# Delta stage of a fused two-block transformer: eight scalings and eight products from VectorE to GpSimd, four key-head projections and two transposes into other PSUM banks

## Chip, cores and metric

The kernel runs on one core of one Trainium2 chip. The metric is the device time of one execution in microseconds (us). Each core has engines that run their own instruction lists in order: TensorE (PE: matmuls and transposes through the PE, with its weight loads as PEld), VectorE (DVE), ScalarE (ACT), GpSimd (POOL) and SyncE (SP), which here issues nearly all DMAs. A matmul writes to one of eight PSUM banks, and VectorE or ScalarE must read a bank out before it is written again.

## The reference

The kernel computes two transformer blocks on 256 tokens of width 1024. The change touches only the last layer, a gated DeltaNet mixer, on 272 positions (16 meta positions ahead of the 256):

```python
def deltanet_mixer(h, norm_w, w_in, conv_w, a_log, dt_bias, o_norm_w, w_out):
    u = rms_norm(h, norm_w) @ w_in
    qkv, z, b, a = jnp.split(u, ...)
    qkv = jax.nn.silu(causal_depthwise_conv(qkv, conv_w))
    ...
    q = jnp.repeat(l2_norm(q...), rep, axis=2)
    k = jnp.repeat(l2_norm(k...), rep, axis=2)
    q = q * (DN_HEAD_DIM_K ** -0.5)
    beta = jax.nn.sigmoid(b)
    g = -jnp.exp(a_log) * jax.nn.softplus(a + dt_bias)
    o = chunked_gated_delta_rule(q, k, v, beta, g)
    o = rms_norm(o, o_norm_w) * jax.nn.silu(z)
    return o @ w_out
```

There are 8 key heads, 8 query heads and 16 value heads of 128. The recurrence runs in chunks: the 16 meta positions, then two chunks of 128 tokens. Each chunk needs, for each value head, the inverse of a unit triangular matrix of 128x128 made of the key products and the decays.

## The kernel before

All of this happens in `delta()`, the last stage, from about 1160 us to the end of the span. Layouts are transposed: features on the 128 partitions, positions along the free axis.

**Projections.** The input projection is cut into 49 weight blocks, here called units. Unit 0 gives the rates b and a, units 1 to 8 the key heads, 9 to 16 the query heads, 17 to 32 the value heads, 33 to 48 the gates z. For each unit `unit()` loads a 128x1024 block (`raw`, a ring of four), splits it into a rounded half `hi` on ScalarE (L269) and a rest `lo` on VectorE (L270; rings of three, so that the halves of unit k+3 wait until TensorE is done with unit k), and `proj_t` runs 24 matmuls (lines L280, L281, L282 in turn) into one bank, `pj_ps`. Units 1 to 8 multiply the unnormalised halves `hh`, `hl`, and their result is scaled afterwards by the row R of reciprocal norms when it is read out (`cpad`, L1310, VectorE). For the others `normalise(k)` makes normalised halves `nh`, `nl` meanwhile: `nt` = h times R (L1253, VectorE), then `split_scaled` (L325 on ScalarE, L326 on VectorE).

**Heads.** `conv_head` reads a unit out, applies a causal convolution of four taps (for key heads one tap goes through ScalarE and a GpSimd addition, L1323; the others are VectorE operations, L1325), and `silu` follows on ScalarE (L1330). `gates` evicts the units 33 to 48 with a silu straight from the bank (`z`, also L1330). The tiles of the raw value heads (`craw`) are two buffers, and the gate tiles `z` reuse them: the gates of units 37 to 40 go where the raw value heads 12 to 15 were.

**Chunks.** `decay`, `between` and `products` make the decays and key products; `attend(c, h0)` multiplies the decays by the queries (L1480) and the key-query products. `values()` also transposes, for four value heads at a time, the raw heads (`tp`, L1571), their meta positions (`tp`, L1577, read out as `va`, L1579) and the meta keys (`tp`, L1582, read out as `ka`), and makes the state S after the meta chunk (`mv`, `vsA`, `mS`).

**Inverse.** `inverse()` is a generator whose steps are put between those of `values()`. It gathers the 32x32 diagonal blocks by way of DRAM (`ab`, L1491), inverts them by 31 steps of substitution on VectorE (`sb_t`, L1222, and `ub`, L1224), sends the result back through DRAM (`e<-ub`, L1496, and eight `U<-e`, L1499), and then, for each of eight groups of four heads, puts the blocks together on TensorE: transposes on VectorE (L1513), products `r` (L1519), `zt` and `z` (L1527, L1531), `r` (L1539), `z` (L1545), with evictions on ScalarE (`pr`, L1522 and L1533; `rn`, L1542) and copies on VectorE between them. `step` and `finish` then run the chunks and the output projection.

**PSUM.** Four pools of two banks each: `pj` (tag "pj") for the projections, `pa`, `pb` and `pk` (tag "b") for all else. Before the change both sorts of meta transposes take banks of `pb`, which also holds `kq`, `mv`, `mS`; `pk` holds `zt` and `z` of L1545, and some of the decays; `pa` holds the key products, `r`, and `z` of L1531.

**Order.** A scheduler orders each engine's list from the program and its own estimates; so an edit in one place can reorder many instructions elsewhere. Waits are then put in where an operation needs another engine's result or a free buffer.

Of the kernel before, what the change touches and what calls it, by code (L numbers as in the profile page):

```python
# [6 lines left out]
F32 = mybir.dt.float32  # L7
# [5 lines left out]
ALU = mybir.AluOpType  # L13
# [177 lines left out]
class Net:  # L191
# [1035 lines left out]
    def delta(self, NZ=2, AH=4, KN=8, SS=1, SR=3, SW=3):  # L1227
        nc, ap = self.nc, self.ap
        ident, tri = self.c("ident"), self.c("tri")
        conv = self.d("conv").rearrange("p (b i) -> p b i", i=4)  # L1230
        h4 = self.h3
        A = self.pool("deA", side="right")
        dr = self.pool("deD", space=bass.MemoryType.DRAM)
        pa = self.pool("pa3", bufs=2, space=PSUM, side="left")
        pb = self.pool("pb3", bufs=2, space=PSUM, side="left")
        pj = self.pool("pj3", bufs=2, space=PSUM, side="right")
        pk = self.pool("pk3", bufs=2, space=PSUM, side="right")
        bank = lambda p, n: p.tile([128, 4, 128], F32, name=n, tag="b")
# [11 lines left out]

        def normalise(k):
            t = W.tile([128, L], F32, name="nt", bufs=2)
            nc.vector.tensor_mul(t, h4[:, k], R)  # L1253
            self.split_scaled(nh[:, k], nl[:, k], t, gd[:, k:k + 1])

        def proj(ts=slice(0, L)):
            ps = pj.tile([128, 512], F32, name="pj_ps", tag="pj")
            n = ts.stop - ts.start
            u = next(units)
            a = (hh, hl) if u <= KN else (nh, nl)  # L1260
            self.proj_t(ps[:, :n], self.unit(ap["w_t3"][u]), (a[0][:, :, ts], a[1][:, :, ts]))
            return ps[:, :n]


        X = Slices(V.tile([128, 2048], F32, name="early", tag="8"))
        bt = X.tile([128, L], F32, name="bat")
        nc.vector.tensor_mul(bt, proj(), R)
        tp = bank(pb, "tp")
        for c in (1, 2, 0):
# [31 lines left out]
        def conv_head(dst, b, t0=0):  # L1301

            n = L - t0
            t = max(t0 - 4, 0)
            w = [conv[:, b, i:i + 1] for i in range(4)]
            ps = proj(slice(t, L))
            src = W.tile([128, L], F32, name="cpad", bufs=2)[:, :L - t]
            early = 8 <= b < 8 + KN
            if early:
                nc.vector.tensor_mul(src, ps, R)  # L1310
                ps = src
            else:
                nc.scalar.activation(src, ps, AF.Copy)
            nc.scalar.activation(dst, ps[:, t0 - t:t0 - t + n], AF.Copy, scale=w[3])  # L1314
            for i in (2, 1, 0):

                o = max(3 - i - t0, 0)
                at = t0 - t - 3 + i + o
                x, y = src[:, at:at + n - o], dst[:, o:]
                if early and i == 2:  # L1320
                    x2 = W.tile([128, L], F32, name="ctap", bufs=2)[:, :n - o]
                    nc.scalar.activation(x2, x, AF.Copy, scale=w[i])
                    nc.gpsimd.tensor_add(y, y, x2)  # L1323
                else:
                    nc.vector.scalar_tensor_tensor(y, x, w[i], y, op0=ALU.mult, op1=ALU.add)  # L1325

        def silu(raw, after=None, src=None):

            with self.tc.issue_after(self.last), self.tc.issue_after(after or self.last):
                return nc.scalar.activation(raw, raw if src is None else src, AF.Silu).ins  # L1330
# [21 lines left out]
        qT = A.tile([128, 8, T], F32, name="qT", tag="q8")  # L1352
# [56 lines left out]
        for j in range(8):  # L1409
            conv_head(kT[:, j], 8 + j)  # L1410
            normalise(j)
            if j == 2:
                cumulate()
            if j in (3, 5, 7):
                silu(kT[:, (0 if j == 3 else j - 1):j + 1])
# [9 lines left out]
        ps = pb.tile([128, 8, M], F32, name="mkk", tag="b")  # L1425
# [31 lines left out]
        for c in range(2):  # L1457
# [6 lines left out]
            for h0 in range(0, 16, 4):  # L1464
# [5 lines left out]
                                        op=ALU.mult)  # L1470
# [3 lines left out]
        def attend(c, h0):  # L1474
            ts = CH[c + 1]
            tq = slice(ts.start - M, ts.stop - M)
            hs = slice(h0, h0 + 4)
            j0 = h0 // 2
            q4 = qg[c][:, hs].rearrange("p (j r) c -> p j r c", r=2)
            nc.vector.tensor_tensor(q4, q4, qT[:, j0:j0 + 2, None, tq].to_broadcast([128, 2, 2, 128]), op=ALU.mult)  # L1480
            ps = bank(pb, "kq")
            for j in range(2):
                nc.tensor.matmul(ps[:, j], kT[:, j0 + j, ts], qT[:, j0 + j, tq], start=j == 0, stop=True,
                                 skip_group_check=True)
            a4 = at[c][:, hs].rearrange("p (j r) c -> p j r c", r=2)
            nc.vector.tensor_tensor(a4, a4, ps[:, 0:2, None, :].to_broadcast([128, 2, 2, 128]), op=ALU.mult)
# [68 lines left out]
        def values():  # L1555
            for j in range(8):
                conv_head(qT[:, j], j, M)
            v.extend(half("v", c) for c in range(2))
            for h0 in range(0, 16, 4):
                hs = slice(h0, h0 + 4)  # L1560
                raw = A.tile([128, 4, L], F32, name="craw", bufs=2)
                for j in range(4):
                    conv_head(raw[:, j], 16 + h0 + j)
                    if h0 and j % 2:
                        attend(j // 2, h0 - 4)
                    yield
                silu(qT[:, h0 // 2:h0 // 2 + 2], silu(raw))
                for c in range(2):
                    tp = bank(pb, "tp")
                    for j in range(4):  # L1570
                        nc.tensor.transpose(tp[:, j], raw[:, j, CH[c + 1]], ident)  # L1571
                    for j in range(0, 4, 2):
                        nc.scalar.activation(v[c][:, h0 + j:h0 + j + 2], tp[:, j:j + 2], AF.Copy,
                                             scale=ri[:, c + 1, (h0 + j) // 2:(h0 + j) // 2 + 1])
                tp = bank(pb, "tp")
                for j in range(4):
                    nc.tensor.transpose(tp[:M, j], raw[:, j, CH[0]], ident)  # L1577
                va = W.tile([M, 4, 128], F32, name="va")
                nc.scalar.activation(va, tp[:M], AF.Copy)  # L1579
                tp = bank(pb, "tp")  # L1580
                for j in range(2):
                    nc.tensor.transpose(tp[:M, j], kT[:, h0 // 2 + j, CH[0]], ident)  # L1582
                ka = W.tile([M, 2, 128], F32, name="ka")
                nc.scalar.activation(ka, tp[:M, 0:2], AF.Copy)
                ps = bank(pb, "mv")
                for j in range(4):
                    nc.tensor.matmul(ps[:M, j], um[:, h0 + j], va[:, j], start=True, stop=True,
                                     skip_group_check=True)
                vs = W.tile([M, 4, 128], F32, name="vsA")
                nc.vector.tensor_tensor(vs, ps[:M], bw[:M, 0, hs, None].to_broadcast([M, 4, 128]), op=ALU.mult)  # L1590
                ps = bank(pb, "mS")
                for j in range(2):
                    nc.tensor.matmul(flat(ps[:, 2 * j:2 * j + 2]), ka[:, j],
                                     flat(vs[:, 2 * j:2 * j + 2]), start=True, stop=True, skip_group_check=True)
                nc.scalar.activation(S[:, hs], ps, AF.Copy)
            for c in range(2):
                attend(c, 12)
                yield
            for h0 in range(0, 4 * NZ, 4):
                z = A.tile([128, 4, T], F32, name="z", tag="craw", bufs=2)  # L1600
                yield from gates(z)
                sz.append(z)
            self.logexp()

        def gates(z):
            for j in range(4):
                silu(z[:, j], src=proj(slice(M, L)))
                yield
# [4 lines left out]
        for _ in values():  # L1613
            next(side, None)
# [113 lines left out]
        op = [o0, o1]  # L1728
# [46 lines left out]
```

## Time and profile before

| | us |
|---|---|
| median of 3 runs | 1471.88 (1471.32 to 1475.75) |
| the profiled execution, its own time | 1471.34 |
| its span in the trace | 1468.7 |
| TensorE busy in the span | 1442.7 (98%) |
| VectorE busy | 1058.8 (72%) |
| ScalarE busy | 793.4 (54%) |
| GpSimd busy | 73.2 (5%) |

The time of the profiled execution is 2.64 us more than its span. Busy shares are over the whole span; the delta stage is the last fifth of it. Line numbers in the trace are those of the kernel; behind the change they are two higher from L1255 on (L1330 becomes L1332, L1513 becomes L1515).

### The profile page before, as it was taken

What the parts mean: (1) busy time and instruction counts of PE and PEld (TensorE: products, weight loads), DVE (VectorE), ACT (ScalarE), POOL (GpSimd) and SP (SyncE); (2) the same over time, 40 slices, a digit from 0 to 9 for tenths busy, and PEclk for the clock granted to TensorE, in tenths of its full rate; (3) what the DMA queues carried; (4) which work ended last, traced back from release to release, by engine and by line L of the source; (5) the groups of instructions that cost most, each with busy time, mean ns of one, the idle gap of its engine ahead of it and who ended that gap; (6) DMA issues with size and microseconds to landing.
All of it is one profiled execution on the core that took longest, in us unless ns stands there. A gap on an engine that the chain in (4) does not pass through costs nothing.

```text
span 1468.7 us, 27090 instructions
## 1 busy us (share of the span) xinstructions
PE 1442.7 (98%) x10635; PEld 1320.6 (90%) x10635; DVE 1058.8 (72%) x2114; ACT 793.4 (54%) x1364; POOL 73.2 (5%) x106
## 2 busy tenths in 40 slices
PE   9999999999999999999999999999999989999998
PEld 8788999999999999999888888888898989899786
DVE  7667577789948888998555555555777688885564
ACT  5566545545544444444444445445686667764464
POOL 0000000000000000000000000000113024000020
PEclk9999999999999999999999999999999999999999
DMA  7452464555665545555666656666442434545113
GB/s 241 131 158 73 146 193 150 171 164 170 198 177 159 161 154 172 157 150 172 191 195 193 194 190 204 190 195 190 154 119 87 144 115 140 164 128 158 33 57 102
DMA packets 72079, 229.19 MB, mean 156 GB/s; under 512 B 16032, under 2 KB 16192, under 8 KB 71952
## 3 DMA queue, kind: packets, MB, share of 16 engines
q1 hardware_dynamic: 71408, 225.82, 50.3%
q8 instruction: 83, 1.36, 0.4%
q0 software_dynamic: 400, 1.46, 0.3%
q14 instruction: 44, 0.36, 0.1%
q10 hardware_dynamic: 144, 0.20, 0.1%
HBM read 225.31 MB, written 2.13 MB: 155 GB/s over the span
## 4 chain that ended last, share of the span: by engine, by line
PE 93%; ACT 2%; DVE 2%; issue 1%; DMA 1%; POOL 0%; SPq 0%; ACTq 0%; DVEq 0%
PE pu_ps L280 10%; PE pu_ps L281 9%; PE pu_ps L282 9%; PE acc L280 8%; PE acc L281 8%; PE acc L282 8%; PE pj_ps L280 8%; PE pj_ps L281 8%; PE pj_ps L282 8%; PE pt_ps L898 2%; PE tr_ps L366 1%; PE out L282 1%; PE out L280 1%; PE out L281 1%; PE sc_ps L652 1%
## 5 line engine op out<-in xcount | busy, mean ns | idle before, releaser
L269 ACT ACTIVATE hi<-raw 128x1024 fp32r<-128x1024 f32 x422 | 445.8, 1058 | 435.8 <-PE pu_ps L281 166.0
L270 DVE TENSOR_TENSOR lo<-raw,hi 128x1024 fp32r<-128x1024 f32 x422 | 517.9, 1228 | 202.2 <-ACT hi L269 201.1
L280 PE MATMUL pu_ps<-x2h,hi 128*128 128x256 f32 x1152 | 330.8, 288 | 0.1
L281 PE MATMUL pu_ps<-x2l,hi 128*128 128x256 f32 x1152 | 326.4, 284 | 0.2 <-DVE x2l L275 0.2
L282 PE MATMUL pu_ps<-x2h,lo 128*128 128x256 f32 x1152 | 325.9, 283 | 0.0
L281 PEld LDWEIGHTS pu_ps<-x2l,hi 128*128 128x128 f32 x1152 | 221.0, 192 | 0.4 <-DVE x2l L275 0.4
L280 PEld LDWEIGHTS pu_ps<-x2h,hi 128*128 128x128 f32 x1152 | 220.5, 192 | 0.3 <-ACT x2h L274 0.3
L282 PEld LDWEIGHTS pu_ps<-x2h,lo 128*128 128x128 f32 x1152 | 220.7, 192 | 0.0
L281 PE MATMUL acc<-lo,ch 128*128 128x512 f32 x512 | 198.8, 389 | 0.0
L282 PE MATMUL acc<-hi,cl 128*128 128x512 f32 x512 | 198.2, 389 | 0.0
L280 PE MATMUL acc<-hi,ch 128*128 128x512 f32 x512 | 139.0, 389 | 0.0
L280 PE MATMUL pj_ps<-hh,hi 128*128 128x256 f32 (+1 forms) x432 | 125.2, 294 | 3.8 <-DVE cpad L1310 2.6
L281 PE MATMUL pj_ps<-hl,hi 128*128 128x256 f32 (+1 forms) x432 | 125.8, 292 | 1.0 <-DVE hl L326 1.0
L282 PE MATMUL pj_ps<-hh,lo 128*128 128x256 f32 (+1 forms) x432 | 125.5, 292 | 0.8 <-DVE lo L270 0.8
L281 PEld LDWEIGHTS acc<-lo,ch 128*128 128x128 f32 x512 | 96.1, 188 | 19.9
L282 PEld LDWEIGHTS acc<-hi,cl 128*128 128x128 f32 x512 | 96.1, 188 | 19.9
L280 PEld LDWEIGHTS acc<-hi,ch 128*128 128x128 f32 x512 | 96.0, 188 | 19.8
L280 PE MATMUL pj_ps<-nh,hi 128*128 128x256 f32 (+2 forms) x320 | 93.4, 292 | 1.6 <-ACT craw L1314 1.5
L281 PE MATMUL pj_ps<-nl,hi 128*128 128x256 f32 (+2 forms) x320 | 92.8, 290 | 0.0
L282 PE MATMUL pj_ps<-nh,lo 128*128 128x256 f32 (+2 forms) x320 | 92.1, 288 | 0.0
L280 PEld LDWEIGHTS pj_ps<-hh,hi 128*128 128x128 f32 x432 | 81.4, 190 | 5.8 <-issue 3.0
L281 PEld LDWEIGHTS pj_ps<-hl,hi 128*128 128x128 f32 x432 | 81.9, 190 | 2.8 <-DVE hl L326 1.9
(558 smaller groups left out, 2413.0 us busy)
## 6 DMA issues: line engine op xcount, KB each, us to landing
raw<-w_u SPq DMA_DIRECT2D x128, 512.0 KB, 3.7
raw<-w_v SPq DMA_DIRECT2D x128, 512.0 KB, 3.6
raw<-w_t SPq DMA_DIRECT2D x106, 512.0 KB, 3.7
raw<-w_o SPq DMA_DIRECT2D x32, 512.0 KB, 3.7
raw<-w_q SPq DMA_DIRECT2D x16, 512.0 KB, 3.7
raw<-w_br SPq DMA_DIRECT2D x8, 512.0 KB, 3.6
raw<-w_c SPq DMA_DIRECT2D x4, 512.0 KB, 3.9
xT<-xT SPq DMA_DIRECT2D x4, 256.0 KB, 5.1
```

Of the source, the lines that this page charges most:

```text
L269: nc.scalar.activation(hi, raw, AF.Copy)
L270: self.residual = (eng or nc.vector).tensor_sub(lo, raw, hi).ins
L280: mm(out, a[0], b[0], start=start, stop=False, **kw)
L281: mm(out, a[0], b[1], start=False, stop=False, **kw)
L282: mm(out, a[1], b[0], start=False, stop=stop, **kw)
L366: nc.tensor.transpose(tp[:, j], b, self.c("ident"))
L652: nc.tensor.matmul(ps[:, j], nq[:, h // 2, ti], kzT[:, 4 * b + 2 * (h // 4) + h % 2, :n], start=j == 0, stop=False, skip_group_check=True)
L898: nc.tensor.matmul(ps[:, j], at[:, r, j // 2, :, j % 2], bt[:, j // 2, :, j % 2], start=j == 0 and r == 0, stop=r == 1, skip_group_check=True)
```

## The change

Three edits, all in `delta()`. The product of h and R in `normalise`, eight times 128x272, is issued on GpSimd, and so is the product of decays and queries in `attend`, eight times 128x512. The projections of units 1 and 4 take a bank of `pk`, those of units 3 and 6 one of `pa`, all others of `pj`. And both meta transposes take banks of `pk` in place of `pb`.

```diff
--- before.py
+++ after.py
@@ -1250,13 +1250,15 @@
 
         def normalise(k):
             t = W.tile([128, L], F32, name="nt", bufs=2)
-            nc.vector.tensor_mul(t, h4[:, k], R)
+            nc.gpsimd.tensor_mul(t, h4[:, k], R)
             self.split_scaled(nh[:, k], nl[:, k], t, gd[:, k:k + 1])
 
         def proj(ts=slice(0, L)):
-            ps = pj.tile([128, 512], F32, name="pj_ps", tag="pj")
             n = ts.stop - ts.start
             u = next(units)
+
+            pool, tag = {1: (pk, "b"), 3: (pa, "b"), 4: (pk, "b"), 6: (pa, "b")}.get(u, (pj, "pj"))
+            ps = pool.tile([128, 512], F32, name="pj_ps", tag=tag)
             a = (hh, hl) if u <= KN else (nh, nl)
             self.proj_t(ps[:, :n], self.unit(ap["w_t3"][u]), (a[0][:, :, ts], a[1][:, :, ts]))
             return ps[:, :n]
@@ -1477,7 +1479,7 @@
             hs = slice(h0, h0 + 4)
             j0 = h0 // 2
             q4 = qg[c][:, hs].rearrange("p (j r) c -> p j r c", r=2)
-            nc.vector.tensor_tensor(q4, q4, qT[:, j0:j0 + 2, None, tq].to_broadcast([128, 2, 2, 128]), op=ALU.mult)
+            nc.gpsimd.tensor_tensor(q4, q4, qT[:, j0:j0 + 2, None, tq].to_broadcast([128, 2, 2, 128]), op=ALU.mult)
             ps = bank(pb, "kq")
             for j in range(2):
                 nc.tensor.matmul(ps[:, j], kT[:, j0 + j, ts], qT[:, j0 + j, tq], start=j == 0, stop=True,
@@ -1572,12 +1574,12 @@
                     for j in range(0, 4, 2):
                         nc.scalar.activation(v[c][:, h0 + j:h0 + j + 2], tp[:, j:j + 2], AF.Copy,
                                              scale=ri[:, c + 1, (h0 + j) // 2:(h0 + j) // 2 + 1])
-                tp = bank(pb, "tp")
+                tp = bank(pk, "tp")
                 for j in range(4):
                     nc.tensor.transpose(tp[:M, j], raw[:, j, CH[0]], ident)
                 va = W.tile([M, 4, 128], F32, name="va")
                 nc.scalar.activation(va, tp[:M], AF.Copy)
-                tp = bank(pb, "tp")
+                tp = bank(pk, "tp")
                 for j in range(2):
                     nc.tensor.transpose(tp[:M, j], kT[:, h0 // 2 + j, CH[0]], ident)
                 ka = W.tile([M, 2, 128], F32, name="ka")
```

The scheduler's order changes with it. Three places matter for what follows.

On VectorE, the end of the substitution: `ub` 128x31 is its last operation, `lo` (L270) belongs to projection units, and the transposes (L1513, behind the change L1515) open the inverse's blocks. Before:

```order
L1222 TENSOR_TENSOR sb_t<-ub,ab 128x60 [waits DVE_49]
L1590 TENSOR_TENSOR vsA<-mv,betaw 16x512 [waits PE_49]
L270 TENSOR_TENSOR lo<-raw,hi 128x1024 [waits DMAHW1_49,Activation_49]
L1224 TENSOR_TENSOR ub<-ub,sb_t 128x30x2 [waits DVE_49]
L1222 TENSOR_TENSOR sb_t<-ub,ab 128x31 [waits DVE_49]
L1224 TENSOR_TENSOR ub<-ub,sb_t 128x31 [waits DVE_49]
L270 TENSOR_TENSOR lo<-raw,hi 128x1024 [waits DMAHW2_49,PE_49,Activation_49]
L1486 TENSOR_TENSOR at_13247<-at_13247,kq 128x512 [waits PE_49]
L1486 TENSOR_TENSOR hh_13616<-hh_13616,kq 128x512 [waits PE_49]
L270 TENSOR_TENSOR lo<-raw,hi 128x1024 [waits DMAHW3_49,Activation_49]
L1513 STREAM_TRANSPOSE pr<-U_13245 32x4x32 [waits DMAHW0_49]
```

Behind the change:

```order
L1224 TENSOR_TENSOR ub<-ub,sb_t 128x30x2 [waits DVE_49]
L270 TENSOR_TENSOR lo<-raw,hi 128x1024 [waits DMAHW7_49,PE_49,Activation_49]
L1222 TENSOR_TENSOR sb_t<-ub,ab 128x31 [waits DVE_49]
L1224 TENSOR_TENSOR ub<-ub,sb_t 128x31 [waits DVE_49]
L270 TENSOR_TENSOR lo<-raw,hi 128x1024 [waits DMAHW0_49,PE_49,Activation_49]
L270 TENSOR_TENSOR lo<-raw,hi 128x1024 [waits DMAHW1_49,PE_49,Activation_49]
L1515 STREAM_TRANSPOSE pr<-U_13245 32x4x32 [waits DMAHW6_49,Pool_49]
L1515 STREAM_TRANSPOSE pr<-U_13245 32x4x32
```

The last `ub` stands one `lo` behind that of unit 39 in the new order, where it stood behind that of unit 41; two `lo` (units 40 and 41) and nothing else are between it and the first transposes.

On TensorE, what stands ahead of unit 39, the third gate unit of the second gate tile. Before (L1582 are the meta keys' transposes of the last four heads, and the rows L280 and L281 at the end open unit 39):

```order
L282 MATMUL pj_ps<-nh_13168,lo 128x256
L1582 MATMUL tp<-cst,kT 16x128 [waits PE_49,Activation_49]
L1582 MATMUL tp<-cst,kT 16x128
L1587 MATMUL mv<-va,um 16x128 [waits Activation_49]
L1587 MATMUL mv<-va,um 16x128 x3
L280 MATMUL pj_ps<-nh_13168,hi 128x256 [waits Activation_49]
L281 MATMUL pj_ps<-nl_13169,hi 128x256
```

Behind the change (L1547 is the last product of the inverse's first block, L1579 the meta transposes of the raw heads, L1533 and L1529 products of the second and third block, and the last row opens unit 39):

```order
L1547 MATMUL z_15065<-U_13245,rn 64x64 [waits DMAHW0_49,Activation_49]
L1547 MATMUL z_15065<-U_13245,rn 64x64 x3
L1579 MATMUL tp<-cst,craw 16x128 x4
L1533 MATMUL z_15136<-U_13245,pr 32x32 [waits Activation_49] x2
L1533 MATMUL z_15136<-U_13245,pr 32x32 x6
L1584 MATMUL tp<-cst,kT 16x128 [waits DVE_49]
L1584 MATMUL tp<-cst,kT 16x128
L1589 MATMUL mv<-va,um 16x128 [waits Activation_49]
L1589 MATMUL mv<-va,um 16x128 x3
L1529 MATMUL zt<-pr,U_13245 32x32 [waits PE_49]
L1529 MATMUL zt<-pr,U_13245 32x32 x3
L280 MATMUL pj_ps<-nh_13168,hi 128x256 [waits Activation_49]
```

The whole first block of the inverse and part of the second, which stood among the units behind 39, now stand between units 38 and 39, and the meta transposes of the last four heads stand behind that first block.

On ScalarE, the same place: `va` reads out the meta transposes, `z` are the silu evictions of the gate units, `hi` (L269) the halves of the units to come. Before:

```order
L1573 ACTIVATE v_14174<-tp,rinv 128x256
L1579 ACTIVATE va<-tp 16x512 [waits PE_49]
L1330 ACTIVATE z<-pj_ps 128x256 [waits Activation_49]
L269 ACTIVATE hi<-raw 128x1024 [waits DMAHW1_49,DVE_49,PE_49]
L1330 ACTIVATE z<-pj_ps 128x256 [waits PE_49]
L1584 ACTIVATE ka<-tp 16x256 [waits PE_49]
L269 ACTIVATE hi<-raw 128x1024 [waits DMAHW2_49,DVE_49,PE_49]
L1330 ACTIVATE z<-pj_ps 128x256 [waits PE_49]
L1595 ACTIVATE S<-mS 128x512 [waits PE_49]
L269 ACTIVATE hi<-raw 128x1024 [waits DMAHW3_49,DVE_49,PE_49]
L1330 ACTIVATE z<-pj_ps 128x256 [waits PE_49]
```

Behind the change:

```order
L269 ACTIVATE hi<-raw 128x1024 [waits DMAHW0_49,DVE_49,PE_49]
L269 ACTIVATE hi<-raw 128x1024 [waits DMAHW1_49,DVE_49,PE_49]
L1524 ACTIVATE pr<-r_14951 32x4x32 [waits PE_49]
L1524 ACTIVATE pr<-r_14951 32x4x32
L1535 ACTIVATE pr<-zt 32x4x32 [waits PE_49]
L1544 ACTIVATE rn<-r_15058 64x256 [waits PE_49]
L1524 ACTIVATE pr<-r_15119 32x4x32 [waits PE_49]
L1524 ACTIVATE pr<-r_15119 32x4x32
L1581 ACTIVATE va<-tp 16x512 [waits PE_49]
L1332 ACTIVATE z<-pj_ps 128x256 x2
L1586 ACTIVATE ka<-tp 16x256 [waits PE_49]
```

The evictions `z` of units 37 and 38, which stood one behind `va` and one behind a further `hi`, now stand together behind `va`, and `va` stands behind the evictions of the inverse's first block (`pr`, `pr`, `rn`).

## Rows read from the trace of the kernel before

**Rows 1.** The profile's page, its first line, its engines, and one group.
```profile
span 1468.7 us, 27090 instructions
...
PE 1442.7 (98%) x10635; PEld 1320.6 (90%) x10635; DVE 1058.8 (72%) x2114; ACT 793.4 (54%) x1364; POOL 73.2 (5%) x106
...
L270 DVE TENSOR_TENSOR lo<-raw,hi 128x1024 fp32r<-128x1024 f32 x422 | 517.9, 1228 | 202.2 <-ACT hi L269 201.1
```

**Rows 2.** Waits of TensorE, 1150 to 1470: the four longest; total us, times, longest us.
```profile
PE pj_ps L280 <- DVE cpad L1310: 2.6, 1, 2.6
...
PE kk L1385 <- ACT kT L1330: 1.7, 1, 1.7
...
PE pj_ps L280 <- ACT craw L1314: 1.5, 1, 1.5
...
PE tp L1582 <- ACT v L1573: 1.4, 1, 1.4
```

**Rows 3.** Timeline of TensorE in unit 6: start, length, operation.
```profile
1184.53 0.43 PE L281 MATMUL pj_ps<-hl,hi 128*128 128x272 f32 x1
...
1184.76 0.43 PE L282 MATMUL pj_ps<-hh,lo 128*128 128x272 f32 x1
...
1187.32 0.29 PE L282 MATMUL pj_ps<-hh,lo 128*128 128x272 f32 x1
...
1187.44 0.29 PE L280 MATMUL pj_ps<-hh,hi 128*128 128x272 f32 x1
```

**Rows 4.** Busy time by stretch: span, engines with counts, granted clock, DMA.
```profile
1180.00:1190.00 10.00, 7.37 (x49) 7.18 (x48) 9.19 (x22) 4.43 (x8) 2.53 (x1) 0.83 0.52 157
...
1360.00:1370.00 10.00, 8.46 (x124) 6.74 (x124) 6.81 (x19) 4.89 (x11) 0.39 (x2) 1.00 0.37 105
```

**Rows 5.** Groups of VectorE, 1150 to 1470: busy, mean ns.
```profile
L1253 DVE TENSOR_TENSOR nt<-h,R 128x272 f32<-128x272 f32 x8 | 3.6, 465 | 0.0
...
L1480 DVE TENSOR_TENSOR qg<-qg,qT 128x512 f32<-128x512 f32 x4 | 2.7, 679 | 0.0
```

**Rows 6.** Groups of GpSimd, 1150 to 1470: busy, mean ns, idle before.
```profile
L1687 POOL TENSOR_TENSOR dsq<-dsq,qT 128x512 f32<-128x512 f32 x8 | 11.6, 1452 | 55.2 <-ACT dsq L1685 55.2
...
L1323 POOL TENSOR_TENSOR kT<-kT,ctap 128x271 f32<-128x271 f32 x8 | 11.0, 1377 | 57.3 <-ACT ctap L1322 57.3
```

**Rows 7.** Timeline of GpSimd, 1422 to 1431.
```profile
1428.02 2.25 POOL L1687 TENSOR_TENSOR dsq<-dsq,qT 128x512 f32<-128x512 f32 x1 [1.31 <-ACT dsq L1685]
```

**Rows 8.** Timeline of VectorE in the same stretch.
```profile
1423.75 0.68 DVE L275 TENSOR_TENSOR o1qg<-v,o1at 128x512 fp32r<-128x512 f32 x1
...
1429.04 1.78 DVE L275 TENSOR_TENSOR o0l<-v,o0h 128x512 fp32r<-128x512 f32 x1
```

**Rows 9.** Timeline of VectorE: first and last step of the substitution, first transposes.
```profile
1251.17 0.19 DVE L1222 TENSOR_TENSOR sb_t<-ub,ab 128x31 f32<-128x31 f32 x1 [1.73 <-DMA ab<-e]
...
1324.03 0.22 DVE L1224 TENSOR_TENSOR ub<-ub,sb_t 128x31 f32<-128x31 f32 x1
...
1331.73 1.53 DVE L1513 STREAM_TRANSPOSE pr<-U 32x128 f32<-32x128 f32 x6
```

**Rows 10.** Timeline of SyncE's queue: the round trip of the solved blocks.
```profile
1324.32 1.50 SPq L1496 DMA_DIRECT2D e<-ub  x1
...
1329.08 4.05 SPq L1499 DMA_DIRECT2D U<-e  x8
```

**Rows 11.** Timeline of ScalarE around units 36 to 39.
```profile
1313.10 1.06 ACT L269 ACTIVATE hi<-raw 128x1024 fp32r<-128x1024 f32 x1 [1.04 <-PE pj_ps L281]
...
1320.08 0.57 ACT L1579 ACTIVATE va<-tp 16x512 f32<-16x512 f32 x1
```

**Rows 12.** Timeline of TensorE: the start of unit 39.
```profile
1321.70 0.39 PE L280 MATMUL pj_ps<-nh,hi 128*128 128x256 f32 x1
```

**Rows 13.** Groups of ScalarE, 1330 to 1365.
```profile
L1522 ACT ACTIVATE pr<-r 32x128 f32<-32x128 f32 x9 | 2.4, 269 | 3.3 <-PE r L1519 3.1
```

**Rows 14.** Groups of TensorE, 1330 to 1365.
```profile
L1519 PE MATMUL r<-pr,U 128*32 128x32 f32 x80 | 2.5, 199 | 0.0
```

## The prediction

> **What bounds the kernel now.** I read the page first: TensorE is busy for 1442.7 of 1468.7 us [rows 1], so there are 26 us of idle time in the whole kernel, and a change that moves work off VectorE or GpSimd is worth only what it takes out of TensorE's idle time, or adds to it. So the second view is TensorE's waits in the delta stage, from 1150 us on. Four of them are over 1 us: 2.6 us for the scaled read-out of a key head (`cpad`), 1.7 us for the first key products, 1.5 us for a value head's read-out, 1.4 us for the meta keys' transposes [rows 2]. Third, the timeline around the longest shows a cost that the list of waits leaves out: behind it the matmuls of unit 6 start 0.23 us apart, and the last ones of the unit 0.12 us apart [rows 3], with a granted clock of 0.83 in that stretch [rows 4]. About twelve matmuls ran at the lower of the two levels (1.2 in place of 2.4 GHz), some 12 x 0.105 = 1.2 us more. Fourth, VectorE in the same stretch is busy for 9.19 of 10 us while TensorE is busy for 7.37 [rows 4]: at the head of the stage VectorE sets the pace, not the banks alone. Last I read the round trip of the solved diagonal blocks, because the new order puts it ahead of unit 39.
>
> **The head of the stage.** With six banks, units 2 to 8 no longer wait for VectorE's read-out of the unit two before. What can be won is 2.6 (`cpad`) + 1.2 (clock) + 1.7 (the key products, which now stand behind unit 8) = 5.5 us. But key heads must still be scaled on VectorE before the convolutions, and unit 9 needs all eight normalised pairs. Eight `nt` of 0.465 us leave VectorE, 3.7 us [rows 5]; they go to GpSimd, where an operation of nearly the same form and width, the addition of L1323, takes 1.38 us on the mean [rows 6]. No row shows `nt` on GpSimd. It costs GpSimd 8 x 1.4 = 11 us beside the 11.0 us of additions, in a stretch of some 33 us, so GpSimd itself has room. What it does to VectorE has a row elsewhere: L275 takes 0.68 us alone and 1.78 us where it meets a GpSimd product of 128x512 [rows 7, 8], 1.1 us more, which for a half as wide operation I put at 0.5. Then eight `nt` give VectorE back 3.7 and take 8 x 0.5 = 4.0 from it. The gain is thus between 0 (VectorE sets the pace as before) and 5.5 us. I take 3.5, on the upper side, because the idle times in the stretch were TensorE's waits for one read-out at a time, which the further banks do spread. **-3.5.**
>
> The page "SBUF — State Buffer" of the Trainium skill, section "Who interferes with whom", says that a VectorE instruction with two SBUF inputs and a GpSimd instruction that reads SBUF exclude each other for a whole instruction. The stretched L275 agrees with it. By that rule alone the head would gain nothing, and the sum below would come out 3.5 us later.
>
> **Queries on GpSimd.** Eight L1480 of 0.679 us, 5.4 us in all, leave VectorE [rows 5], and come to GpSimd as the same form as L1687, 1.45 us on the mean and 2.25 in one that met VectorE [rows 6, 7]. GpSimd has nothing else to do then. VectorE gets back 5.4 us and loses up to 8 x 1.1 = 8.8 us where they meet. This counts only for when the substitution ends, below.
>
> **Meta transposes.** In `pk` they no longer wait for `pb`: the 1.4 us of L1582 [rows 2] goes. **-1.4.** The wait of 1.5 us for a value head's read-out is a matter of ScalarE's order; it may go or stay (0 to -1.5). I take a third. **-0.5.**
>
> **What is late next.** The banks of `pk` are also those of the inverse's `zt` and L1547, and the scheduler has put the meta transposes of the last four heads behind the inverse's first block. The evictions `z` of units 37 and 38 write into the buffer that these transposes read, and stand behind `va` on ScalarE; they free both banks of `pj`, which units 39 and 40 need, since only key heads got other banks. So unit 39 waits for this chain: last `ub` of the substitution, DMA to DRAM, DMAs back, transposes on VectorE, the first block, meta transposes, `va`, two `z`. Its length:
>
> The last `ub` waits for `lo` of unit 39, which waits for `hi` of unit 39, which waits for the end of unit 36: `hi` 1.06, `lo` 1.23 and the last pair of operations at 0.2 each come to 2.7, with hand-overs 2.9 us [rows 1, 9, 11]. From the last `ub` to the end of the first transposes: before, it ended at 1324.25, the DMA to DRAM was issued at 1324.32, the DMAs back at 1329.08, the transposes began at 1331.73 and took 1.5 us [rows 9, 10], 9.0 us in all; of these I take off 0.6 because a `lo` stood in the way. 8.4 us. Then the block: six steps on TensorE and five small evictions on ScalarE of 0.27 [rows 13], `va` at 0.57 [rows 11], and a `z`; with matmuls of 0.2 us [rows 14] and a hand-over of 0.1 to 0.2 at each of a dozen changes of engine I estimate 5.4 to 6.4 us, and take 6.0. So unit 39 starts 2.9 + 8.4 + 6.0 = 17.3 us behind the end of unit 36. Before, it started at 1321.70 [rows 12], 8.6 us behind the end of unit 36, which released `hi` at 1313.10 [rows 11]. The stretch is 8.7 us longer. It now holds work of the inverse that stood behind unit 39: about 60 small matmuls, of which 80 of L1519 were busy for 2.5 us [rows 14], so 1.9 us at that rate and up to 3.1 with the gaps between them. Net 5.6 to 6.8 us; I take 6.2. **+6.2.** Units 37 and 38 lie inside it, nothing else can fill it, because the list of TensorE is in order.
>
> An idle time of some 8 us is longer than the 2.6 us behind which the clock fell; I add the same price again. **+1.2** (0 if the small matmuls hold the clock).
>
> The chain starts later if VectorE has not finished 31 steps by then. The substitution took from 1251.17 to 1324.25, 73 us [rows 9]. It now starts about 7 us earlier (one unit of 3 us earlier in the order, and the head's gain), at 1244. Its stretch loses 5.4 us of products and two `lo` of 1.23, and wins up to the 8.8 us of overlap: 65 to 74 us, so it ends at 1309 to 1318. TensorE's bound is 1313.1 less what has been gained by then (5.4), plus 2.9: 1310.6. So 0 to 7 us; nearer the lower end, since VectorE idled in that stretch and the overlaps will seldom be full. **+1.5.**
>
> **The tail.** From 1360 to 1370 TensorE idled for 1.5 us between small steps of the inverse and of `step` [rows 4]; now projections are left over that stand between them. Between 0 and -1.5, **-1.0.**
>
> **Sum.** -3.5 - 1.4 - 0.5 + 6.2 + 1.2 + 1.5 - 1.0 = +2.5. The profiled execution took 1471.34 us (its span and 2.64), so 1473.8; the median of the runs shown is 0.5 above that execution, and I forecast 1474.0 us. The lower ends add to -5.5 - 1.4 - 1.5 + 5.6 - 1.5 = -4.3, time 1467.0; the upper ones to -1.4 + 6.8 + 1.2 + 7 = +13.6, time 1485.
>
> **Rivals.** The first ends faster: GpSimd takes sixteen operations without slowing VectorE, so the head gains all 5.5, the substitution is never late and the clock holds through the small matmuls. That is the lower sum, 1467.0. Speaks for it: the idle times at the head are waits for banks. Against: the stall ahead of unit 39 follows from the order alone. It decides where the head's gain passes 5 us and the stall stays under 6.
>
> The second ends slower: GpSimd's reading holds VectorE up whenever they meet. The head gains nothing (+3.5 on the sum), and six of the eight products fall into the substitution at 1.1 - 0.68 = 0.4 to 1.1 us net each, on a VectorE that is then the bound: the lateness goes from 1.5 to about 5. 1474 + 3.5 + 3.5 = 1481. It decides where the substitution ends behind 1315. The same rule of the Trainium skill as above ("SBUF — State Buffer", "Who interferes with whom") would bring this about; the trace shows single stretched operations, not how many.
>
> The third is GpSimd's own queue: `nt` and the additions of L1323 share one in-order list, and the sixteen take 22 us at the mean of 1.4 but 36 us at the 2.25 of an operation that was held up [rows 6, 7]. Then unit 9 waits for the last `nl`, some 3 us later than before in place of 3.5 earlier: 1480.
>
> **Chances and range.** My forecast (1470 to 1478) 0.45, the first rival 0.22, the second 0.25, the third 0.08. A difference under 0.3%, 4.4 us, can hardly be told from none here, so the bounds are 1467.5 and 1476.3. Of the forecast's 0.45 about 0.36 lies within, 0.07 above and 0.02 below; of the first rival 0.16 is below 1467.5; the others are above. Faster 0.18, same 0.42, slower 0.40. The range runs from the first rival's 1466 to the second's 1482.
>
> **What would show it.** Units 2 to 8 without a wait for `cpad`, and the start of unit 10 some 3 us earlier; no wait at the meta transposes; a stall of 7 to 9 us right ahead of unit 39, in pieces, which the waits give to `z`, `va`, `pr` and the transposes; the last `ub` 2.9 us behind unit 36 or later; VectorE's L1325 and L270 longer where GpSimd runs. The forecast is wrong if unit 39 starts right behind unit 38, or if the GpSimd products take under 1 us and stretch nothing.

## The result: slower by 0.67%

The changed kernel took 1482.3 us (median of 5 runs, 1480.51 to 1483.02) against 1471.88 us for the kernel before: a ratio of 1.0067, 95% interval [1.0052, 1.0081]. The forecast of 1474.0 us had the sign and the place of the loss, but a fifth of its size, and 1482.3 lies 0.3 us past the end of its range (the upper ends of its terms add up to 1485). The kernel before took 1469 to 1473 us in 55 of its 76 executions in the comparisons below, and 1474 to 1477 us in the other 21, with a granted clock over the span of 0.992 to 0.995 in these and 0.996 to 0.999 in those, so that its median there is 1470.5 to 1470.8.

Its profiled execution has a span of 1481.2 us, 12.5 us more than before. TensorE's waits from 1150 us on, the longest of them (total, times, longest, us), which answer to [rows 2]:

```profile
PE r L1521 <- DMA U<-e: 6.4, 1, 6.4
PE kk L1387 <- ACT kT L1332: 2.7, 1, 2.7
PE pj_ps L280 <- DVE cpad L1312: 2.2, 2, 1.4
PE pj_ps L280 <- ACT qT L1316: 1.4, 1, 1.4
...
PE r L1521 <- DVE pr L1515: 0.8, 1, 0.8
```

The 1.4 us of the meta keys' transposes is gone, and a wait of 6.4 us for the DMAs of the solved blocks has come. At the head of the stage 2.6 + 1.7 us have become 2.7 + 2.2 us, with 0.8 us for a `lo`. The 1.4 us for `qT`, at 1241, stand where the 1.5 us for `craw` stood. The waits alone do not add up to 12.5 us. The busy times by stretch (columns as in [rows 4]; the granted clock is the third number from the right) show the rest:

```profile
1190.00:1200.00 10.00, 5.91 (x38) 5.50 (x37) 9.15 (x20) 7.11 (x10) 3.69 (x4) 0.82 0.54 181
1200.00:1210.00 10.00, 10.00 (x85) 9.66 (x83) 6.45 (x21) 6.16 (x12) 0.93 (x1) 0.84 0.20 59
1320.00:1330.00 10.00, 2.84 (x30) 2.56 (x30) 4.50 (x11) 1.53 (x2) 0.00 (x0) 0.81 0.69 200
1330.00:1340.00 10.00, 9.58 (x113) 7.05 (x110) 3.35 (x10) 3.46 (x11) 0.20 (x1) 0.50 0.28 70
1340.00:1350.00 10.00, 10.00 (x103) 8.95 (x101) 3.47 (x7) 3.59 (x7) 0.20 (x1) 0.84 0.01 2
```

At the head the clock falls in unit 9, the first query head. Its first matmuls before (start, length, idle time before):

```profile
1197.53 0.39 PE L280 MATMUL pj_ps<-nh,hi 128*128 128x260 f32 x1
1197.76 0.28 PE L281 MATMUL pj_ps<-nl,hi 128*128 128x260 f32 x1
1197.88 0.28 PE L282 MATMUL pj_ps<-nh,lo 128*128 128x260 f32 x1
```

Behind the change:

```profile
1197.73 0.58 PE L280 MATMUL pj_ps<-nh,hi 128*128 128x260 f32 x1 [1.40 <-DVE cpad L1312]
1198.11 0.42 PE L281 MATMUL pj_ps<-nl,hi 128*128 128x260 f32 x1
1198.33 0.42 PE L282 MATMUL pj_ps<-nh,lo 128*128 128x260 f32 x1
```

It starts 0.2 us later than before, and its matmuls follow each other at 0.22 us in place of 0.12.

From 1320 to 1330 TensorE works for 2.8 us. From 1330 to 1340 it is busy for 9.6 us at a granted clock of 0.50, the lower level, and the clock is back only in the stretch after. The timeline of TensorE there:

```profile
1328.76 0.29 PE L1521 MATMUL r<-pr,U 128*32 128x32 f32 x2 [6.41 <-DMA U<-e]
1329.80 0.61 PE L1521 MATMUL r<-pr,U 128*32 128x32 f32 x14 [0.75 <-DVE pr L1515]
```

```profile
1336.46 1.89 PE L1589 MATMUL mv<-va,um 16*16 16x128 f32 x8
...
1338.84 0.58 PE L280 MATMUL pj_ps<-nh,hi 128*128 128x256 f32 x1
1339.22 0.42 PE L281 MATMUL pj_ps<-nl,hi 128*128 128x256 f32 x1
1339.44 0.41 PE L282 MATMUL pj_ps<-nh,lo 128*128 128x256 f32 x1
```

The products of `mv`, eight in the trace, take 1.89 us, unit 39 starts at 1338.84, 17.1 us later than before [rows 12], and its matmuls are 0.22 us apart. The chain that it waits for reads on VectorE, on SyncE's queue and on ScalarE, which answer to [rows 9 to 11]:

```profile
1319.12 1.22 DVE L270 TENSOR_TENSOR lo<-raw,hi 128x1024 fp32r<-128x1024 f32 x1
...
1320.49 0.22 DVE L1224 TENSOR_TENSOR ub<-ub,sb_t 128x31 f32<-128x31 f32 x1
...
1328.04 1.63 DVE L1515 STREAM_TRANSPOSE pr<-U 32x128 f32<-32x128 f32 x6 [3.46 <-DMA U<-e]
```

```profile
1320.78 0.38 SPq L1498 DMA_DIRECT2D e<-ub  x1
...
1325.95 4.04 SPq L1501 DMA_DIRECT2D U<-e  x8
```

```profile
1315.70 1.06 ACT L269 ACTIVATE hi<-raw 128x1024 fp32r<-128x1024 f32 x1 [1.20 <-issue]
...
1335.47 0.59 ACT L1581 ACTIVATE va<-tp 16x512 f32<-16x512 f32 x1 [1.42 <-PE tp L1579]
1335.97 0.62 ACT L1332 ACTIVATE z<-pj_ps 128x256 f32<-128x256 f32 x2
```

`hi` of unit 39 starts at 1315.70 with the end of unit 36, the last `ub` ends at 1320.71, the DMAs back are issued at 1325.95, the transposes start at 1328.04, `va` ends at 1336.06 and the two `z` at 1336.59. So the banks are free some 2 us before unit 39 starts; in between TensorE is busy with what stands ahead of it in its list (`mv` and products of the third block).

### The profile page after: what moved, and what is told of

Read it like the earlier page. It is cut to its first block, busy times and chain, and to the rows that moved or that the text cites. A ratio compares the mean times of both kernels' runs of the same rounds, so it can differ in the third digit from the quotient of the medians.

```text
span 1481.2 us, 27080 instructions
## 1 busy us (share of the span) xinstructions
PE 1448.8 (98%) x10635; PEld 1327.5 (90%) x10635; DVE 1060.0 (72%) x2098; ACT 794.4 (54%) x1365; POOL 89.5 (6%) x122
## 4 chain that ended last, share of the span: by engine, by line
PE 90%; DVE 5%; ACT 2%; DMA 1%; issue 1%; SPq 0%; ACTq 0%; DVEq 0%
PE pu_ps L280 9%; PE pu_ps L281 9%; PE pu_ps L282 9%; PE acc L280 8%; PE acc L282 8%; PE acc L281 8%; PE pj_ps L282 7%; PE pj_ps L280 7%; PE pj_ps L281 7%; PE pt_ps L898 2%; DVE lo L270 2%; PE tr_ps L366 1%; PE out L282 1%; PE out L280 1%; PE out L281 1%
## 5 line engine op out<-in xcount | busy, mean ns | idle before, releaser
L269 ACT ACTIVATE hi<-raw 128x1024 fp32r<-128x1024 f32 x422 | 445.6, 1057 | 440.5 <-PE pu_ps L281 166.1
L270 DVE TENSOR_TENSOR lo<-raw,hi 128x1024 fp32r<-128x1024 f32 x422 | 519.3, 1232 | 203.3 <-ACT hi L269 200.6
L280 PE MATMUL pu_ps<-x2h,hi 128*128 128x256 f32 x1152 | 331.1, 288 | 0.1
L281 PE MATMUL pu_ps<-x2l,hi 128*128 128x256 f32 x1152 | 326.6, 284 | 0.2 <-DVE x2l L275 0.2
L281 PEld LDWEIGHTS pu_ps<-x2l,hi 128*128 128x128 f32 x1152 | 221.1, 192 | 0.4 <-DVE x2l L275 0.4
L280 PEld LDWEIGHTS pu_ps<-x2h,hi 128*128 128x128 f32 x1152 | 220.6, 192 | 0.3 <-ACT x2h L274 0.3
L281 PE MATMUL acc<-lo,ch 128*128 128x512 f32 x512 | 198.9, 389 | 0.0
L280 PE MATMUL acc<-hi,ch 128*128 128x512 f32 x512 | 139.0, 390 | 0.0
L280 PE MATMUL pj_ps<-hh,hi 128*128 128x256 f32 (+1 forms) x432 | 125.2, 294 | 2.5 <-ACT hi L269 1.6
L281 PE MATMUL pj_ps<-hl,hi 128*128 128x256 f32 (+1 forms) x432 | 125.8, 292 | 0.7 <-DVE hl L326 0.6
L281 PEld LDWEIGHTS acc<-lo,ch 128*128 128x128 f32 x512 | 96.1, 188 | 19.9
L280 PEld LDWEIGHTS acc<-hi,ch 128*128 128x128 f32 x512 | 96.0, 188 | 19.8
L280 PE MATMUL pj_ps<-nh,hi 128*128 128x256 f32 (+2 forms) x320 | 95.0, 297 | 3.7 <-ACT qT L1316 1.4
L281 PE MATMUL pj_ps<-nl,hi 128*128 128x256 f32 (+2 forms) x320 | 94.4, 295 | 0.0
L280 PEld LDWEIGHTS pj_ps<-hh,hi 128*128 128x128 f32 x432 | 81.6, 190 | 4.5 <-ACT hi L269 2.0
L282 PEld LDWEIGHTS pj_ps<-hh,lo 128*128 128x128 f32 x432 | 82.0, 190 | 3.4 <-DVE lo L270 2.0
```

Of the source, the lines that this page charges most:

```text
L269: nc.scalar.activation(hi, raw, AF.Copy)
L270: self.residual = (eng or nc.vector).tensor_sub(lo, raw, hi).ins
L280: mm(out, a[0], b[0], start=start, stop=False, **kw)
L281: mm(out, a[0], b[1], start=False, stop=False, **kw)
L282: mm(out, a[1], b[0], start=False, stop=stop, **kw)
```

## The experiments

All of them ran against the kernel before, and "before" is its median in the same comparison. Parts are named (a) `nt` on GpSimd, (b) the banks of units 1, 3, 4 and 6, (c) the queries' product on GpSimd, (d) the meta transposes in `pk`. The theory: (d) ties unit 39 to the inverse's first block, and the clock behind that stall adds to it; what is left of the loss is the head. The rival: GpSimd's reads hold VectorE up, and the stall is only where that shows.

**Without (d).** The changed kernel with both transposes in the old pool (this line stands twice).

```diff
-                tp = bank(pk, "tp")
+                tp = bank(pb, "tp")
```

> The changed kernel with the two meta transposes back in pool pb, the rest kept. Theory (the meta transposes in pk tie the gate evictions, and so unit 39, to the inverse's first block; the half clock behind that stall makes it longer): the stall ahead of unit 39 and the slow clock behind it go, and what is left is the head, which came out 2.4 us later than before in the changed kernel: 1472 to 1476 us. Rival (GpSimd's reads slow VectorE, and the stall is only where it shows): no better than 1480.

1474.89 us, before 1470.80: 1.0032 [1.0018, 1.0046]. More than half of the loss is gone with (d); the rival's 1480 is excluded.

**(d) alone.** Only these two lines in the kernel before, the other way round.

> The kernel before with only the two meta transposes moved to pk. Theory (they tie unit 39 to the inverse's first block): a stall of 6 us or more ahead of unit 39 with a granted clock near 0.5 behind it, and 1478 to 1482 us. Rival (GpSimd is the cause): the wait of 1.4 us at the transposes goes and nothing comes for it, 1470.5.

1483.37 us: 1.0085 [1.0070, 1.0101], 1.4 us past the expected range. (d) alone costs at least what the whole change costs (1.0067 [1.0052, 1.0081]). Its longest wait, and busy time by stretch:

```profile
PE r L1519 <- DMA U<-e: 11.2, 1, 11.2
```

```profile
1320.00:1330.00 10.00, 0.92 (x16) 0.68 (x16) 3.88 (x16) 0.23 (x1) 0.00 (x0) 0.50 0.61 152
1330.00:1340.00 10.00, 9.79 (x102) 7.40 (x103) 3.07 (x10) 3.23 (x11) 0.20 (x1) 0.50 0.04 7
1340.00:1350.00 10.00, 10.00 (x101) 8.79 (x101) 3.70 (x8) 3.74 (x8) 0.20 (x1) 0.82 0.01 2
```

No GpSimd product takes part in it (the busy POOL column is 0.00 and 0.20 us). TensorE works for 0.92 us in the ten from 1320 on.

**Three groups of four.** (d) alone, but the last group of value heads keeps its old banks (this line, too, stands twice).

```diff
-                tp = bank(pk, "tp")
+                tp = bank(pk if h0 < 12 else pb, "tp")
```

> The kernel before with the meta transposes of the first three groups of value heads in pk, those of the last group left in pb. Theory (what costs is that the last group's transposes, which hold the buffer of the gates of units 37 to 40, queue behind the inverse's first block for a bank of pk): no stall ahead of unit 39, 1468 to 1473 us against 1483.4 with all four groups moved. Rival (any meta transpose in pk disturbs the inverse and the decays): 1477 or more.

1468.89 us, before 1470.48: 0.9984 [0.9971, 0.9997]. The stall is gone, and so are the 1.4 us at the meta keys' transposes; its waits begin with:

```profile
PE pj_ps L280 <- DVE cpad L1310: 2.6, 1, 2.6
PE pj_ps L280 <- ACT craw L1314: 1.5, 1, 1.5
PE kk L1385 <- ACT kT L1330: 1.4, 1, 1.4
```

So the stall needs the last of the four groups, the one whose transposes hold the buffer of the gates of units 37 to 40. That this buffer is the tie is read from the program and from the order; no run gave the gates a buffer of their own.

**The clock.** (d) alone with 36 idle transposes on TensorE, which wait for the last `ub` and fill the time of the DMAs behind it. They write to a bank that nothing reads, so that nothing that is computed changes.

```diff
+            warm = bank(pa, "warm")
+            for i in range(36):
+                nc.tensor.transpose(warm[:, i % 4], ub[...], ident)
```

> The meta move alone, with 36 more transposes of the solved blocks on TensorE, into a bank that nothing reads, between the end of the substitution and the inverse's first product, in time that TensorE waits for DMAs anyway. Theory (a good part of the price is the lower clock behind the stall, some 14 us of small products and of unit 39 at half speed): the clock is up again when the first product starts, and the kernel is 3 to 6 us faster than the meta move alone: 1477 to 1480 us. Rival (the chain behind the stall waits for hand-overs, not for the clock, or the clock does not come back in that time): 1482 to 1485.

1478.16 us, before 1470.48: 1.0045 [1.0029, 1.0061], against 1.0085 without the filling. With 36 matmuls more the kernel is 5.2 us faster (1483.37 - 1478.16). In its trace, TensorE's stretch from 1330 and two pieces of its timeline:

```profile
1330.00:1340.00 10.00, 9.82 (x130) 7.94 (x130) 3.05 (x9) 3.39 (x11) 0.20 (x1) 1.00 0.06 10
```

```profile
1322.66 6.38 PE L1508 MATMUL warm<-cst,ub 128*128 128x128 f32 x36 [5.46 <-DVE ub L1224]
...
1333.86 1.04 PE L1590 MATMUL mv<-va,um 16*16 16x128 f32 x8
...
1335.20 0.39 PE L280 MATMUL pj_ps<-nh,hi 128*128 128x256 f32 x1
```

The granted clock is 1.00 where it was 0.50. `mv` takes 1.04 in place of 1.89 us, and unit 39 starts at 1335.20, 3.0 us earlier than in (d) alone, although the substitution ends at the same place (1322.52 us, 1322.39 without the filling).

**(b) alone.**

```diff
+            pool, tag = {1: (pk, "b"), 3: (pa, "b"), 4: (pk, "b"), 6: (pa, "b")}.get(u, (pj, "pj"))
```

> The kernel before with only the banks of units 1, 3, 4 and 6 changed. Theory (with nt on VectorE nothing stretches, and the waits for one read-out at a time are spread): unit 10 starts 2 to 5 us earlier than before, 1467 to 1470 us. Rival (VectorE's work sets the pace of the head, whatever the banks): within 1.5 us of before.

1477.98 us, before 1470.80: 1.0046 [1.0033, 1.0059]. Neither: the banks alone cost 7 us. Its waits, and four of its stretches:

```profile
PE pj_ps L280 <- DVE cpad L1312: 3.7, 1, 3.7
PE pj_ps L280 <- ACT qT L1316: 3.0, 1, 3.0
...
PE cum L1336 <- DVE gdec L1290: 1.2, 1, 1.2
```

```profile
1180.00:1190.00 10.00, 6.99 (x56) 6.76 (x54) 10.00 (x19) 5.66 (x9) 2.57 (x2) 1.00 0.49 157
1190.00:1200.00 10.00, 8.38 (x54) 8.10 (x54) 8.54 (x23) 6.88 (x11) 2.43 (x3) 0.83 0.36 107
1200.00:1210.00 10.00, 9.33 (x60) 8.41 (x60) 5.88 (x18) 5.95 (x13) 1.26 (x1) 0.66 0.16 52
1240.00:1250.00 10.00, 8.51 (x55) 8.51 (x56) 6.61 (x10) 5.54 (x13) 3.82 (x6) 0.83 0.88 229
```

TensorE runs ahead through units 2 to 7 (unit 7 ends at 1186.99 us, before at 1191.77) and then stands for 3.7 us, up to 1190.68, where it stood for 2.6 us before; VectorE is busy for 10.00 us from 1180 to 1190. The wait of 3.0 us for `qT`, at 1241, stands where 1.5 us for `craw` stood. So the two waits are longer than before, and the clock is low in three stretches (0.83, 0.66 and 0.83) where it was in one.

**(a) alone and (c) alone, then both.**

```diff
-            nc.vector.tensor_mul(t, h4[:, k], R)
+            nc.gpsimd.tensor_mul(t, h4[:, k], R)
```

> The kernel before with only the eight products of h and R moved to GpSimd. Theory (each of them takes from VectorE more than it gives back): VectorE busy longer at the head, unit 10 starts 1 to 4 us later, 1473 to 1476 us. Rival (VectorE is relieved by 8 times 0.35 us): 1469 to 1471.

1469.91 us, before 1470.80: 0.9991 [0.9980, 1.0002]. No difference that this measurement tells; the time is the rival's, the reason is not. From 1168 to 1200 VectorE is busy for 28.7 us, for 28.8 before, though eight operations have left it: `nl` takes 0.69 us in place of 0.49, and the key heads' convolutions (L1325) 0.64 in place of 0.56.

```diff
-            nc.vector.tensor_tensor(q4, q4, qT[...], op=ALU.mult)
+            nc.gpsimd.tensor_tensor(q4, q4, qT[...], op=ALU.mult)
```

> The kernel before with only the eight products of decays and queries on GpSimd. Theory (GpSimd's reads hold VectorE up by about what it saves, so the substitution ends no earlier, and the order puts the inverse's first product ahead of unit 39): within 2 us of before or up to 4 us slower, 1470 to 1475. Rival (VectorE is relieved by 5 us there, and the kernel is bound by it): 1466 to 1469.

1474.14 us, before 1470.48: 1.0015 [1.0004, 1.0026]. Two steps of the substitution beside two products, on VectorE and on GpSimd:

```profile
1304.47 0.40 DVE L1224 TENSOR_TENSOR ub<-ub,sb_t 128x231 f32<-128x231 f32 x1
1304.90 1.40 DVE L1222 TENSOR_TENSOR sb_t<-ub,ab 128x220 f32<-128x220 f32 x1
1306.34 1.33 DVE L1224 TENSOR_TENSOR ub<-ub,sb_t 128x220 f32<-128x220 f32 x1
...
1308.73 0.36 DVE L1222 TENSOR_TENSOR sb_t<-ub,ab 128x207 f32<-128x207 f32 x1
```

```profile
1304.79 1.27 POOL L1480 TENSOR_TENSOR qg<-qg,qT 128x512 f32<-128x512 f32 x1 [11.54 <-ACT qT L1330]
1306.02 1.40 POOL L1480 TENSOR_TENSOR hl<-hl,qT 128x512 f32<-128x512 f32 x1
```

An operation of about 0.38 us takes 1.3 to 1.4 us beside a product of 1.3 to 1.4 us; each of these two products so takes about 1.0 us from VectorE, and gives it 0.68. Even so the last `ub` ends 5.9 us earlier than before (1318.38 for 1324.25), with a changed order. In this trace the meta keys' transposes wait 3.6 us for a `v`, and from 1310 to 1320 the granted clock is 0.79, for 1.00 before; the convolutions that now stand behind steps of the substitution may be what makes the `v` late.

> Both moves to GpSimd, banks and meta transposes as before. Theory (the moves to GpSimd are neutral, and all of the loss is that of the banks): 1469 to 1474 us. Rival (GpSimd's reads add up): 1476 or more.

(a) and (c) together: 1469.90 us, before 1470.48: 0.9988 [0.9977, 0.9999]. The loss of (c) alone is not there, with another order. How much of it was the reads and how much the order stays open.

**What is left, and a better kernel.** The changed kernel with the last group's transposes in `pb`; the changed kernel with all units in `pj`; and (a), (a) and (c), each with three groups in `pk` and the old banks.

> The changed kernel with one difference: the meta transposes of the last group in pb. Theory (the last group is the whole stall; the banks' loss of some 4 us at the head stays): 1471 to 1476 us. Rival (several parts of the change make the stall together): 1478 or more.

1473.16 us: 1.0011 [1.0001, 1.0021], against 1.0067 with that group moved.

> The changed kernel with all projections in pool pj, as before; the meta transposes and both moves to GpSimd kept. Theory (the stall stays whole, the head's loss goes): 1478 to 1481 us. Rival (the banks are what pushes unit 39 behind the inverse): 1472 or less.

1478.66 us: 1.0050 [1.0033, 1.0067]. The stall stays without the banks. This kernel differs from (d) alone by (a) and (c) only, and is 4.7 us faster (1483.37 - 1478.66). The last `ub` in (d) alone, and then here:

```profile
1322.18 0.21 DVE L1224 TENSOR_TENSOR ub<-ub,sb_t 128x31 f32<-128x31 f32 x1
```

```profile
1316.90 0.22 DVE L1224 TENSOR_TENSOR ub<-ub,sb_t 128x31 f32<-128x31 f32 x1
```

> The products of h and R on GpSimd and the meta transposes of the first three groups in pk; banks and queries as before. Theory (each is worth about 1 to 2 us and they are in different places): 1466 to 1469 us, faster than before. Rival (the head's order decides, and the two do not add): 1469 to 1472.

1467.82 us: 0.9977 [0.9965, 0.9989].

> As the one before, with the queries' products on GpSimd too, which put the inverse's first product at unit 40 and not 43. Theory (with three groups in pk the first product is not waited for): 1466 to 1470 us. Rival (the inverse's first product waits, as it did for the queries alone): 1472 to 1475.

1468.03 us: 0.9974 [0.9961, 0.9986]. Before was 1470.57 in these four. Both last kernels are faster than the kernel before by about 0.25%; the queries' place makes no difference between them.

## Why the forecast had the place and not the size

**The head (forecast -3.5).** This is the step that failed. The forecast took the waits for single read-outs as something that more banks spread. They gather them instead. Units 6 to 8 do run ahead (unit 8 ends at 1192.48 us, before at 1197.65), but the key products behind them wait 2.7 us and unit 9 another 1.4 us for VectorE's `cpad`, so that unit 9 starts where it started. The clock, whose 1.2 us in unit 6 the forecast counted as won, then is low through nearly all of unit 9, which takes 5.6 us in place of 3.1. So its end, which releases `hi` of unit 12, came 2.4 us later than before (1203.12 for 1200.68). The term was wrong by 5.9 us. (b) alone shows the loss without GpSimd, and in the changed kernel with all units in `pj` that `hi` starts at 1200.38. The sentence of the forecast that VectorE sets the pace of the head was right, and the gain of 3.5 us contradicted it. `nt` on GpSimd took 0.91 us and not 1.4:

```profile
L1253 POOL TENSOR_TENSOR nt<-h,R 128x272 f32<-128x272 f32 x8 | 7.2, 911 | 36.7 <-ACT R L235 34.1 <-DVE nl L326 2.6
```

```profile
L326 DVE SCALAR_TENSOR_TENSOR nl<-nt,dat_sb,nh 128x272 fp32r<-128x272 f32 x8 | 4.8, 608 | 0.0
```

but `nl` beside it went from 0.49 to 0.61 us, and in (a) alone VectorE's total for the head stayed what it was (28.7 for 28.8 us). By the rule on the shared port pair (the Trainium skill, "SBUF — State Buffer", "Who interferes with whom"), the head gains nothing from (a); the trace (`nl`) and the run of (a) alone (1469.91 for 1470.80 us) agree.

**Ahead of unit 39.** The chain was the right one, up to `va`; its last hop was TensorE's own list and not the two `z`. From the end of unit 36 to the last `ub`: 5.0 us (1315.70 to 1320.71), where 2.9 + 1.5 were forecast. That the 1.5 fits is in part luck: the substitution started 8 us later than forecast (1252.21 for 1244), and the end of unit 36 came 8 us later too, against which the term counts. From there to the first block's products: 9.1 us, forecast 8.4. From these (1329.80) to unit 39 (1338.84): 9.0 us, forecast 6.0. In (d) alone it is 9.2 us (1329.04 to 1338.23), and with the filling 6.2 (1328.97 to 1335.20), so the excess is the clock.

**The clock (forecast +1.2).** Too small by 4 us: 5.2 us by the filled run, of which 3.0 are in the block and some 2.3, by estimate, in unit 39 (24 matmuls 0.21 us apart in (d) alone, 0.12 with the filling). That run is of (d) alone, but the changed kernel has the same block 2.8 us longer than the filled one, and unit 39 at 0.22. The forecast carried over the price of twelve matmuls, half a projection unit. Behind this stall the lower level lasted some 14 us, through the inverse's products, the state of the meta chunk and unit 39, as the stretches at 0.50 and 0.84 show. How long it lasts was not to be had from [rows 3], where a projection followed at once.

**The wait of 1.4 us and the tail (forecast -1.4, -0.5 and -1.0).** The first went, as forecast. The second stayed: 1.4 us for `qT` in place of 1.5 for `craw`. The tail gave back more: unit 39 started 17.1 us late and the span grew by 12.5 us, so 4.6 us came back behind it, of which 1.9 to 3.1 were forecast as work of the inverse done early, and 1.0 as the tail.

**Sum.** Forecast and result are 8.3 us apart by the medians, and 10.0 by the spans (+12.5 for +2.5). Of the 10.0, 8.0 arise up to the end of unit 36, which came 2.6 us later (1315.70 for 1313.10) where -3.5 - 1.4 - 0.5 put it 5.4 earlier: 5.9 are the head; the 1.9 us to be won behind it do not show, though the wait of 1.4 us is gone, and where they were lost again was not traced. From there to unit 39 it took 14.5 us more than before, where 8.7 + 1.5 + 1.2 = 11.4 were forecast: 3.1. Behind unit 39, 4.6 us came back where 2.5 + 1.0 were forecast: -1.1.

**The rivals.** The second gave 1481 us, near the result, and its sign came true (the substitution ends behind 1315, at 1320.71), but by another mechanism: VectorE was held up, and the head gained nothing, yet (d) alone has the whole loss without any GpSimd product, and its substitution ends later still, at 1322.39. The first needed a gain of over 5 us at the head. The third needed 36 us for the sixteen operations of GpSimd; they took 15.4 (7.2 and 8.2), and unit 9 started 0.2 us late and not 3.

The parts do not add: alone, (b) and (d) cost 0.46% and 0.85%, and the whole change 0.67%. The stall is why, as far as the traces tell: it ends with the substitution, so TensorE waits the less there the later it comes. In (d) alone unit 38 ends at 1317.07 and TensorE waits 11.2 us; in the changed kernel it ends at 1322.35, the wait is 6.4 us, and unit 39 starts only 0.6 us later (1338.84 for 1338.23). And (a) and (c), which without (d) are worth next to nothing (0.9988), are worth 4.7 us where the substitution is in the way.

## What to carry to other kernels

Before moving a tile to another PSUM pool, follow who frees that pool's banks in the new order, and what the moved read-out itself sets free: here one group of transposes held a buffer that the next projections' read-outs were to write. Where TensorE idles for several us, price the work behind the gap at the lower clock until a trace shows it back, not the gap alone; idle matmuls in a wait that can't be removed paid 5 us here. More banks ahead of a VectorE that was full did not bring unit 9 forward here; the waits only moved together, and the clock fell behind them. What a move is worth depends on what else is in the way: the same products on GpSimd gave next to nothing without the stall and 4.7 us with it.

## What was not expected

The same wait did not always lower the clock. In the run of (d) alone, where the head's order is that of before, TensorE waits 2.6 us for the same `cpad`, and the stretch from 1180 to 1190 has a granted clock of 1.00, for 0.83 before [rows 4]:

```profile
1180.00:1190.00 10.00, 7.32 (x57) 6.94 (x56) 9.69 (x22) 5.73 (x10) 2.52 (x1) 1.00 0.50 157
```

Its `hi` of unit 12 came 1.0 us earlier than before (1199.67 for 1200.68) with the head's order unchanged. The stretch is at 1.00 in the filled run and in that of three groups too, behind the same wait of 2.6 us, and at 0.83 in that of (c) alone. A cost of the clock read from one profiled execution can so be there or not in the next.
